# A hand-made TensorE order for 32 experts: the small products go into one block inside the next expert's first product

## The chip, the core and the metric

The kernel runs on one core of one Trainium2 chip. The metric is the device time of one execution in microseconds, as the median of several runs. A core has five engines with a queue of instructions each: TensorE (PE; its weight loads are shown as PEld), VectorE (DVE), ScalarE (ACT), GpSimd (POOL) and SyncE (SP), which here starts the loads. Each engine takes its own queue in order; between engines semaphores make one wait for another. TensorE reads SBUF and writes PSUM, which has eight banks of 128 partitions x 512 fp32 numbers; every tile of PSUM here is one bank.

## The reference

One decoder layer for 256 tokens of width 1024. A mixing part (gated DeltaNet, stick-breaking attention, cross-attention) comes first. The change touches the second part, a mixture of experts:

```python
logits = x @ w_router + b_router            # 32 experts, each token takes its best 4
gate = softmax(top 4 of logits)
for each expert e, for the tokens that chose it:
    hid = x @ w_gate_up[e] + b_gate_up[e]   # 1024 -> 2048
    glu, lin = min(hid[:, :1024], 7), clip(hid[:, 1024:], -7, 7)
    act = glu * sigmoid(1.702 * glu) * (lin + 1)
    y += gate * (act @ w_down[e] + b_down[e])   # 1024 -> 1024
x = layer_norm(2 ** 0.25 * x + y)
```

All is fp32. The weights of one expert are 12 MB (2 to the 20th bytes each), of all 32 experts 384 MB; each is read once.

## The kernel before

The mixing part takes about the first 355 us. The change is in what follows, the experts, in `tile_layer`.

**Loads.** The weights come in pieces of 128 partitions x 2048 numbers, 1 MB (1.0486 million bytes): eight for the first product of an expert (`wu`, one for each 128 rows of the 1024), four for the second (`wd`). SyncE starts them in a fixed order, the eight of expert e and then the four of expert e-1, into a ring of 21 buffers (`slots["ring"]`: tags of several pools, the last eight added just ahead of the experts). A load waits until the products that read its buffer's old piece are done. Line 829 issues them all.

**One expert.** It has 64 slots for tokens. With e the expert:

- `gather` makes, for two experts at a time (even e), `xg`: products of x with a 0/1 matrix `g2` put the chosen tokens' columns in place (`ps_xg`, two banks' worth, one after the other), and ScalarE and VectorE move each of eight slices out with LayerNorm's scale and bias. `xg` has one buffer for both experts.
- `gemm1` puts the biases into two banks, `glu` (`pg`) and `lin` (`pl`), through products with a selecting matrix `sel` (line 1169), and adds, for each of eight pieces, four products of 64 output partitions (line 1173). The 64 slots fill half of the array's columns, so the products go in pairs for the two halves of a bank; a pair runs side by side. The activation on VectorE and ScalarE follows (`eg`, `es`, `el`).
- `turned` transposes the activation (`pt`, copied to `aT`), and makes from ranks and gates the matrix `gT` and the column `gs` for the way back (`pq`). `pt` and `pq` share the bank `misc`, which has one buffer.
- `gemm2` puts the output bias into the bank `o` (`po`, line 1212) and adds the second product (line 1215), 16 products for four pieces. ScalarE and VectorE make of it the scaled halves `oh` and `ol`.
- `scatter` adds them to the tokens' rows: eight products `y` into four banks that stay for all experts (line 1230).

Experts 5 and 7 hold the residual as well (`residual`, `add_residual`), expert 31 the rows of the last LayerNorm (`ln2_rows`).

**What sets TensorE's order.** The loop at the end of the MoE part writes expert e's `gemm1` with two calls inside (`between`: `scatter(e-2)` behind the first piece, `turned(e-1)` behind the second), and then `gemm2(e-1)`. But a scheduler orders each engine's instructions by its own idea of their times, so what stands in TensorE's queue differs from the text and from expert to expert.

**The branch.** At e = 23 (`IFAT`), after the loads of expert 24 and `scatter(22)`, the kernel reads the largest number of tokens of an expert. If it is over 64, a loop handles the further slots; in these runs it is not. All engines stand at this branch until the others have come.

Of the kernel before, what the change touches and what calls it, by code (L numbers as in the profile page):

```python
# [17 lines left out]
P = 128  # L18
# [15 lines left out]
def tile_layer(ctx, tc, x, xT, memT, w_in, w_convT, a_log, dt_bias, gdn_norm_w, w_mem_kv, w_p_gdn, w_p_sb,  # L34
# [1100 lines left out]
    XG, ACT, SEL, TU, YO = {}, {}, {}, {}, {}  # L1135
# [5 lines left out]
    def gather(e, rcol):  # L1141
        g2 = ew.tile([P, 2, 2, 64], F32, name=f"g2_{e}", tag="g2")
# [6 lines left out]
        for q in range(2):  # L1149
            ps = psg.tile([P, 4, P], F32, name=f"ps_xg{e}{q}", tag=("misc", "o")[q])  # L1150
# [14 lines left out]
    def gemm1(e, sel, between=()):  # L1165
        pg = psg.tile([P, 512], F32, name=f"pg{e}", tag="glu")
        pl = psg.tile([P, 512], F32, name=f"pl{e}", tag="lin")
        for t, ps in enumerate((pg, pl)):
            nc.tensor.matmul(ps, sel, bias[:, t, :], start=True, stop=False)  # L1169
        outs = [(pg, 0), (pg, 1), (pl, 0), (pl, 1)]  # L1170
        for k in range(KT):
# [3 lines left out]
            if k < len(between):  # L1175
                between[k]()
# [32 lines left out]
    def gemm2(e, sel):  # L1209
        aT, gT, gs = TU.pop(e)  # L1210
        po = psg.tile([P, 512], F32, name=f"po{e}", tag="o")
        nc.tensor.matmul(po, sel, bias[:, 2, :], start=True, stop=False)  # L1212
        for ft in range(8):
            for h in range(2):
                nc.tensor.matmul(po[64 * h:64 * h + 64, :], aT[:, ft % 4, ft // 4, :],  # L1215
                                 WD[e][ft // 2].rearrange("p (a c) -> p a c", a=2)[:, ft % 2, 512 * h:512 * h + 512],
                                 start=False, stop=(ft == 7))
        oh = ew.tile([P, 512], F32R, name=f"oh{e}", tag="e3", bufs=3)
# [43 lines left out]
    def ln2_rows():  # L1262
# [4 lines left out]
        return ln2  # L1267
# [18 lines left out]
    def further_slots():  # L1286
# [16 lines left out]
        with tc.For_i(0, -(-T // cap) - 1, 1):  # L1303
            with tc.For_i(0, nexp, 1) as er:
# [15 lines left out]
                gather("o", rc[:, :, None].to_broadcast([P, 2, 2]))  # L1320
                gemm1("o", osel)
                WD["o"] = [down_piece("o", k, er) for k in range(4)]
                turned("o", rc, [gc[:, i:i + 1] for i in range(2)])
                gemm2("o", osel)
# [6 lines left out]
    for e in range(nexp + 1):  # L1331
        load(e)
        if e == IFAT:
            load(e + 1)
        if e < nexp:
            if e % 2 == 0:
                gather(e, rank[:, :, e:e + 2])
            SEL[e] = spread(brs[:, e, :], f"sel{e}")
            if e in (5, 7):
                residual((e - 5) // 2)  # L1340
            between = [lambda: scatter(e - 2)] if e - 2 in YO else []
            if e:
                between.append(lambda: turned(e - 1, rank[:, :, e - 1], [G[:, i, e - 1:e] for i in range(2)]))
            gemm1(e, SEL[e], between)
            if e in (5, 7):
                add_residual((e - 5) // 2)
        else:
            scatter(e - 2)
            turned(e - 1, rank[:, :, e - 1], [G[:, i, e - 1:e] for i in range(2)])
        if e == 0:  # L1350
            gates_of()
        if e == nexp - 1:
            ln2 = ln2_rows()
        if e:
            gemm2(e - 1, SEL[e - 1])
        if e == 2:
            rmi = largest_count()
        if e == IFAT:
            scatter(e - 1)
# [60 lines left out]
```

## Time and profile before

| | |
|---|---|
| median of 3 runs | 1327.99 us (1327.63 to 1331.89) |
| the profiled execution by its own time | 1330.67 us |
| its span in the trace | 1328.9 us |
| TensorE busy | 1262.2 us, 95% of the span |
| VectorE, ScalarE, GpSimd busy | 30%, 21%, 8% |
| bytes read from HBM | 451.35 MB |
| mean granted TensorE clock | 0.991 |

In the views an instruction has the line of the kernel, the engine, the operation, and the tiles out<-in by the program's names. A product of 64 output partitions shows as two records in the trace. In a timeline rows of one kind are merged (x4); in square brackets stands how long the engine was idle before the row and who ended that. In the table of waits, the waiter stands before the arrow and the one waited for behind it. GB/s counts all that the core's 16 DMA engines moved.

### The profile page before, as it was taken

To read this page: it belongs to the slowest core of one execution; us is meant where nothing else is said; L and a number is where in the kernel's file an instruction comes from. 1 tells how busy PE (TensorE), PEld (TensorE's weight loads), DVE (VectorE), ACT (ScalarE), POOL (GpSimd) and SP (SyncE) were. 2 spreads that over 40 slices of the span, in tenths; PEclk is the share of its full clock that TensorE was granted. 3 is DMA by queue.
4 is the path that set the end of the run, shared out by engine and by line. 5 is a ranking of instruction groups with operands and counts; after the bars stand their busy time and mean duration, and the time that the engine had idled before them with its cause. 6 is when DMAs were issued, how large, how long until landed. Compare 5 with 4: busy or idle time off the path is not lost. (4 is left out here: it accounts for less than half of the span.)

```text
span 1328.9 us, 16802 instructions
## 1 busy us (share of the span) xinstructions
PE 1262.2 (95%) x7039; PEld 682.1 (51%) x7039; DVE 400.3 (30%) x692; ACT 276.8 (21%) x448; POOL 99.8 (8%) x156
## 2 busy tenths in 40 slices
PE   7999999999999999999999999999999899999995
PEld 7998889999734433333333333333333244333331
DVE  6875646557412111111111111111121121111203
ACT  5565537445301101010100011010100011010111
POOL 4223313001000000000000000000000000000001
PEclk9999999999999999999999999999999999999998
DMA  7542337867699999999999999999999699999960
GB/s 238 177 142 74 117 135 224 305 191 289 258 418 422 424 422 423 421 413 415 422 420 419 422 424 424 421 423 422 422 423 424 263 389 422 425 421 424 423 278 32
DMA packets 117135, 453.54 MB, mean 341 GB/s; under 512 B 7440, under 2 KB 47456, under 8 KB 84288
## 3 DMA queue, kind: packets, MB, share of 16 engines
q1 hardware_dynamic: 116096, 450.39, 84.3%
q0 software_dynamic: 960, 2.04, 0.6%
q8 instruction: 57, 0.93, 0.3%
q14 instruction: 22, 0.18, 0.0%
HBM read 451.35 MB, written 1.05 MB: 340 GB/s over the span
## 5 line engine op out<-in xcount | busy, mean ns | idle before, releaser
L1173 PE MATMUL pg<-wu,xg 128*64 128x512 f32 x1024 | 316.3, 604 | 0.0
L1173 PE MATMUL pl<-wu,xg 128*64 128x512 f32 x1024 | 306.8, 593 | 0.0
L1215 PE MATMUL po<-wd,aT 128*64 128x512 f32 x1024 | 231.7, 597 | 0.0
L1173 PEld LDWEIGHTS pl<-wu,xg 128*64 128x64 f32 x1024 | 86.6, 137 | 145.8 <-issue 145.7
L1215 PEld LDWEIGHTS po<-wd,aT 128*64 128x64 f32 x1024 | 68.8, 136 | 127.3 <-issue 117.3
L1173 PEld LDWEIGHTS pg<-wu,xg 128*64 128x64 f32 x1024 | 75.7, 136 | 106.0 <-issue 87.5
L1180 DVE TENSOR_SCALAR eg<-pg 128x512 f32<-128x512 f32 x32 | 22.1, 692 | 341.9 <-PE pg L1173 341.9
L68 ACT ACTIVATE es<-eg 128x512 f32<-128x512 f32 x32 | 20.2, 631 | 470.0 <-DVE eg L1180 470.0
L1221 DVE SCALAR_TENSOR_TENSOR ol<-po,gs,oh 128x512 fp32r<-128x512 f32 x32 | 24.0, 750 | 219.9 <-ACT oh L1220 219.8
L1272 POOL CAST sel<-brs 128x128 fp32r<-128x128 f32 x32 | 11.4, 357 | 886.9 <-PE po L1212 886.3
L1154 PEld LDWEIGHTS ps_xg<-g,x 128*128 128x128 f32 x512 | 63.7, 201 | 27.7 <-issue 21.9
L1154 PE MATMUL ps_xg<-g,x 128*128 128x128 f32 x512 | 70.2, 291 | 2.9 <-DVE gs L1206 2.7
L1220 ACT ACTIVATE oh<-po,gs 128x512 fp32r<-128x512 f32 x32 | 22.0, 687 | 244.2 <-PE po L1215 244.2
L1204 DVE CAST gT<-pq 128x256 fp32r<-128x256 f32 x32 | 13.6, 424 | 147.2 <-PE pq L1202 147.2
L1230 PE MATMUL y<-oh,gT 64*128 64x512 f32 x128 | 34.5, 463 | 22.2 <-ACT oh L1220 22.2
L1230 PEld LDWEIGHTS y<-oh,gT 64*128 64x128 f32 x128 | 13.5, 184 | 68.6 <-ACT oh L1220 45.1
L1161 ACT ACTIVATE xg<-ps_xg,l1T 128x128 f32<-128x128 f32 x64 | 29.1, 454 | 77.3 <-PE ps_xg L1154 57.1
L1163 DVE TENSOR_SCALAR xg<-ps_xg,l1T 128x128 f32<-128x128 f32 x64 | 26.1, 408 | 35.7 <-ACT xg L1161 34.9
L1193 ACT COPY aT<-pt 128x512 f32<-128x512 f32 x32 | 18.6, 580 | 46.5 <-PE pt L1191 46.5
L1191 PEld LDWEIGHTS pt<-ident,el 128*128 128x128 f32 x128 | 13.4, 140 | 28.2 <-DVE xg L1163 9.7
L1230 PE MATMUL y<-ol,gT 64*128 64x512 f32 x128 | 27.6, 414 | 0.2
L1181 DVE TENSOR_SCALAR el<-pl 128x512 f32<-128x512 f32 x32 | 22.1, 691 | 5.3 <-PE pl L1173 5.3
(580 smaller groups left out, 1737.1 us busy)
## 6 DMA issues: line engine op xcount, KB each, us to landing
wu<-in_w_gate_up_dram SPq DMA_DIRECT2D x256, 1024.0 KB, 10.3
wd<-in_w_down_dram SPq DMA_DIRECT2D x127, 1024.0 KB, 11.1
wg<-in_w_in_dram SPq DMA_DIRECT2D x12, 1024.0 KB, 5.6
wo<-in_w_o_dram SPq DMA_DIRECT2D x4, 1024.0 KB, 5.1
wk<-in_w_in_dram SPq DMA_DIRECT2D x2, 1024.0 KB, 6.0
wv<-in_w_in_dram SPq DMA_DIRECT2D x2, 1024.0 KB, 5.2
wsq<-in_w_in_dram SPq DMA_DIRECT2D x2, 1024.0 KB, 5.8
wsk<-in_w_in_dram SPq DMA_DIRECT2D x2, 1024.0 KB, 5.1
```

Of the source, the lines that this page charges most:

```text
L68: o = nc.scalar.activation(out, in_, func, **kw)
L1154: nc.tensor.matmul(ps[:, k, :], x1[:, i, d * P:(d + 1) * P], g2[:, i].rearrange("p a b -> p (a b)"), start=(i == 0), stop=(i == 1))
L1161: nc.scalar.activation(dst, ps[:, k, :], AF.Identity, scale=g, bias=b)
L1163: nc.vector.tensor_scalar(dst, ps[:, k, :], g, b, op0=OP.mult, op1=OP.add)
L1173: nc.tensor.matmul(ps[64 * h:64 * h + 64, :], XG[e][:, k, :], WU[e][k][:, 512 * c:512 * c + 512], start=False, stop=(k == KT - 1))
L1180: nc.vector.tensor_scalar(g, pg, 7.0, None, op0=OP.min)
L1181: nc.vector.tensor_scalar(l, pl, 7.0, -7.0, op0=OP.min, op1=OP.max)
L1193: nc.scalar.copy(aT.rearrange("p j a b -> p j (a b)"), pt)
L1215: nc.tensor.matmul(po[64 * h:64 * h + 64, :], aT[:, ft % 4, ft // 4, :], WD[e][ft // 2].rearrange("p (a c) -> p a c", a=2)[:, ft % 2, 512 ...
L1220: nc.scalar.activation(oh, po, AF.Copy, scale=gs)
L1221: nc.vector.scalar_tensor_tensor(ol, po, gs, oh.bitcast(F32), op0=OP.mult, op1=OP.subtract)
L1230: nc.tensor.matmul(yps[i][h], gT[64 * h:64 * h + 64, i, :], o[64 * h:64 * h + 64, :], start=(e == 0 and n == 0), stop=(e == nexp - 1 and n ...
```

## The change

TensorE's queue is now written by hand: the loop stands in `tc.manual_schedule(engines={PE})`, which keeps TensorE's instructions in the order of the text; the other engines are ordered as before. The functions become generators, so that the loop can put one's work between the steps of another:

- Biases: `up_bias(e+1)` stands behind `gemm2(e-1)`, the output bias inside `turned`.
- One block behind the second weight piece of `gemm1(e)`: the transposes `pt`, `scatter(e-2)`, the output bias, `pq`. For e = 5 and 7 the scatter stands behind the first piece, with the residual.
- The gather for experts e+1 and e+2 (odd e): its first half ahead of `gemm2(e-1)`, the second behind that product's second weight piece. Both halves use `misc`; before, the second used `o`. The first gather, and the one behind the branch, stand undivided.
- `largest_count` moves from e = 2 to e = 0, `ln2_rows` between the pieces of the last `gemm1`.

```diff
-            ps = psg.tile([P, 4, P], F32, name=f"ps_xg{e}{q}", tag=("misc", "o")[q])
+            ps = psg.tile([P, 4, P], F32, name=f"ps_xg{e}{q}", tag="misc")
...
-    def turned(e, rc, gates):
+    def turned(e, sel, rc, gates, between=None):
         pt = psg.tile([P, 4, P], F32, name=f"pt{e}", tag="misc")
         for j in range(4):
             nc.tensor.transpose(pt[:, j, :], ACT[e][:, j * P:(j + 1) * P], ident)
+        if between:
+            between()
         aT = ew.tile([P, 4, 2, 64], F32, name=f"aT{e}", tag="e3", bufs=3)
         nc.scalar.copy(aT.rearrange("p j a b -> p j (a b)"), pt)
+        PO[e] = po = psg.tile([P, 512], F32, name=f"po{e}", tag="o")
+        nc.tensor.matmul(po, sel, bias[:, 2, :], start=True, stop=False)
...
+    with tc.manual_schedule(engines={mybir.EngineType.PE}):
...
+                for k in gemm1(e):
+                    if k == 0 and e in (5, 7):
+                        scatter(e - 2)
+                        residual((e - 5) // 2)
+                    if k == 1 and e:
+                        turn_down(e - 1)
...
+                if e % 2 and e + 1 < nexp and e != IFAT:
+                    nxt = pair(e + 1)
+                    next(nxt)
...
+                for k in gemm2(e - 1):
+                    if nxt and k == 1:
+                        next(nxt)
+            if e == IFAT:
+                scatter(e - 1)
+                with tc.If(nc.values_load(rmi[0:1, 0:1], min_val=0, max_val=T) > cap):
+                    further_slots()
+                for _ in pair(e + 1):
+                    pass
+            if e + 1 < nexp:
+                up_bias(e + 1, SEL[e + 1])
```

`turn_down(e)` calls `turned(e, ...)` with `scatter(e-1)` as `between`. Two places of TensorE's queue follow. First, behind the last piece of expert 9's first product. The names: `pg10`, `pl10` gate and linear sums of expert 10, `po8` the output of expert 8, `wd8_0` its first down piece, `ps_xg101` the second half of the gather for experts 10 and 11. Before:

```order
L1169 MATMUL pg10_5177<-bias_2348,sel10_5175 128x512
L1169 MATMUL pl10_5178<-bias_2348,sel10_5175 128x512
L1215 MATMUL po8_5100<-wd8_0_5020,aT8_5055 64x512 x4
L1191 MATMUL pt9_5197<-ident_133,el9_5094 128x128 x4
L1215 MATMUL po8_5100<-wd8_1_5022,aT8_5055 64x512 x4
L1215 MATMUL po8_5100<-wd8_2_5024,aT8_5055 64x512 x4
L1215 MATMUL po8_5100<-wd8_3_5026,aT8_5055 64x512 x4
L1230 MATMUL y00_3821<-oh8_5118,gT8_5064 128x512
L1230 MATMUL y01_3822<-oh8_5118,gT8_5064 128x512
L1230 MATMUL y10_3823<-oh8_5118,gT8_5064 128x512
L1173 MATMUL pg10_5177<-wu10_0_5122,xg_10_5148 64x512
L1154 MATMUL ps_xg101_5162<-g2_10_5146,x1_2139 128x128 x8
```

and now:

```order
L1155 MATMUL ps_xg100_5107<-g2_10_5104,x1_2139 128x128 x8
L1223 MATMUL po8_5059<-wd8_0_5028,aT8_5057 64x512 x4
L1223 MATMUL po8_5059<-wd8_1_5030,aT8_5057 64x512 x4
L1155 MATMUL ps_xg101_5130<-g2_10_5104,x1_2139 128x128 x8
L1223 MATMUL po8_5059<-wd8_2_5032,aT8_5057 64x512 x4
L1223 MATMUL po8_5059<-wd8_3_5034,aT8_5057 64x512 x4
L1170 MATMUL pg10_5155<-bias_2348,sel10_5120 128x512
L1170 MATMUL pl10_5156<-bias_2348,sel10_5120 128x512
L1178 MATMUL pg10_5155<-wu10_0_5159,xg_10_5106 64x512 x2
L1178 MATMUL pl10_5156<-wu10_0_5159,xg_10_5106 64x512 x2
L1178 MATMUL pg10_5155<-wu10_1_5161,xg_10_5106 64x512 x2
L1178 MATMUL pl10_5156<-wu10_1_5161,xg_10_5106 64x512 x2
```

The transposes `pt9` and the `y` of expert 8 no longer stand here; the gather stands whole around two pieces of the down product, and no gate product stands without its partner. Second, the first pieces of expert 10, where the rest of the small products stands. Before:

```order
L1230 MATMUL y11_3824<-oh8_5118,gT8_5064 128x512
L1230 MATMUL y00_3821<-ol8_5119,gT8_5064 128x512
L1230 MATMUL y01_3822<-ol8_5119,gT8_5064 128x512
L1230 MATMUL y10_3823<-ol8_5119,gT8_5064 128x512
L1230 MATMUL y11_3824<-ol8_5119,gT8_5064 128x512
L1173 MATMUL pg10_5177<-wu10_1_5124,xg_10_5148 64x512 x2
L1173 MATMUL pl10_5178<-wu10_1_5124,xg_10_5148 64x512 x2
L1200 MATMUL pq9_5204<-ident_133,gg9_5205 128x128 x2
L1202 MATMUL pq9_5204<-G_221,gg9_5205 128x1 x2
L1173 MATMUL pg10_5177<-wu10_2_5126,xg_10_5148 64x512 x2
L1173 MATMUL pl10_5178<-wu10_2_5126,xg_10_5148 64x512 x2
L1212 MATMUL po9_5247<-bias_2348,sel9_5028 128x512
```

and now:

```order
L1195 MATMUL pt9_5191<-ident_133,el9_5098 128x128 x4
L1240 MATMUL y00_3821<-oh8_5151,gT8_5068 128x512
L1240 MATMUL y01_3822<-oh8_5151,gT8_5068 128x512
L1240 MATMUL y10_3823<-oh8_5151,gT8_5068 128x512
L1240 MATMUL y11_3824<-oh8_5151,gT8_5068 128x512
L1240 MATMUL y00_3821<-ol8_5152,gT8_5068 128x512
L1240 MATMUL y01_3822<-ol8_5152,gT8_5068 128x512
L1240 MATMUL y10_3823<-ol8_5152,gT8_5068 128x512
L1240 MATMUL y11_3824<-ol8_5152,gT8_5068 128x512
L1201 MATMUL po9_5206<-bias_2348,sel9_4986 128x512
L1208 MATMUL pq9_5208<-ident_133,gg9_5209 128x128 x2
L1210 MATMUL pq9_5208<-G_221,gg9_5209 128x1 x2
```

Transposes, all eight `y` of expert 8, the output bias of expert 9 and `pq9` are one block between pieces 1 and 2.

## Rows read from the trace of the kernel before

**Rows 1.** The page: the span, and GB/s in its 40 slices.

```profile
span 1328.9 us, 16802 instructions
...
GB/s 238 177 142 74 117 135 224 305 191 289 258 418 422 424 422 423 421 413 415 422 420 419 422 424 424 421 423 422 422 423 424 263 389 422 425 421 424 423 278 32
```

**Rows 2.** Stages: length; busy us of PE, PEld, DVE, ACT, POOL; granted clock; DMA share; GB/s.

```profile
370.00:470.00 100.00, 99.97 (x488) 39.55 (x486) 21.04 (x43) 11.87 (x20) 0.89 (x3) 1.00 1.02 423
470.00:600.00 130.00, 125.02 (x589) 49.69 (x587) 23.55 (x46) 10.83 (x20) 1.48 (x5) 1.00 1.01 420
600.00:1045.00 445.00, 424.93 (x1985) 159.78 (x1983) 76.55 (x152) 38.94 (x73) 6.15 (x15) 1.00 1.02 422
1045.00:1075.00 30.00, 25.10 (x126) 12.68 (x122) 6.77 (x13) 3.73 (x7) 0.00 (x0) 0.89 0.52 210
1075.00:1275.00 200.00, 195.01 (x916) 73.65 (x917) 35.15 (x69) 18.15 (x33) 2.31 (x7) 1.00 1.02 423
1275.00:1329.00 54.00, 36.71 (x180) 14.59 (x176) 13.77 (x29) 6.38 (x10) 4.20 (x4) 0.90 0.24 94
```

**Rows 3.** Timeline of TensorE, 630 to 700: start us, us, then the instructions.

```profile
636.42 0.47 PE L1169 MATMUL pg<-bias,sel 128*128 128x512 f32 x1
...
646.29 0.73 PE L1230 MATMUL y<-oh,gT 64*128 64x512 f32 x3 [0.85 <-ACT oh L1220]
646.96 1.07 PE L1173 MATMUL pg<-wu,xg 128*64 128x512 f32 x2
647.96 2.05 PE L1154 MATMUL ps_xg<-g,x 128*128 128x128 f32 x16
...
666.40 0.47 PE L1169 MATMUL pg<-bias,sel 128*128 128x512 f32 x1
...
696.02 0.47 PE L1169 MATMUL pg<-bias,sel 128*128 128x512 f32 x1
```

**Rows 4.** Waits of the load queue, 700 to 1000: us in total, times, longest.

```profile
SPq L829 <- PE pl L1173: 173.1, 80, 6.2
```

**Rows 5.** Loads, 600 to 1000: count, KB each, median us from issue to landing.

```profile
wu<-in_w_gate_up_dram SPq DMA_DIRECT2D x111, 1024.0 KB, 9.5
```

**Rows 6.** Waits of the load queue, 1075 to 1275.

```profile
SPq L829 <- DMA wu<-in_w_gate_up_dram: 56.4, 35, 2.1
```

**Rows 7.** Loads, 1080 to 1260.

```profile
wu<-in_w_gate_up_dram SPq DMA_DIRECT2D x48, 1024.0 KB, 19.6
```

**Rows 8.** Timeline around the branch, 1045 to 1075, TensorE and the load queue.

```profile
1050.99 7.04 PE L1215 MATMUL po<-wd,aT 128*64 128x512 f32 x32
...
1064.21 4.51 SPq L829 DMA_DIRECT2D wu<-in_w_gate_up_dram  x8
...
1064.39 0.77 PE L1169 MATMUL pg<-bias,sel 128*128 128x512 f32 x1 [4.00 <-PEq L1360]
```

**Rows 9.** Timeline of TensorE, 1300 to 1329: the last down product.

```profile
1307.01 7.09 PE L1215 MATMUL po<-wd,aT 128*64 128x512 f32 x32
```

**Rows 10.** Timeline of TensorE, 400 to 460: experts 2 to 4.

```profile
403.48 0.48 PE L1169 MATMUL pg<-bias,sel 128*128 128x512 f32 x1
...
409.57 1.07 PE L1173 MATMUL pg<-wu,xg 128*64 128x512 f32 x2
410.57 0.44 PE L1200 MATMUL pq<-ident,gg 128*128 128x128 f32 x2
...
429.20 0.47 PE L1169 MATMUL pg<-bias,sel 128*128 128x512 f32 x1
...
458.47 0.48 PE L1169 MATMUL pg<-bias,sel 128*128 128x512 f32 x1
```

**Rows 11.** Timeline of TensorE, 1275 to 1290: a turnaround of `misc`.

```profile
1280.83 0.93 PE L1258 MATMUL ps_l<-lnr,ident 32*128 32x128 f32 x6 [0.68 <-ACT ln L1266]
```

**Rows 12.** The page, costliest groups: busy us, mean ns, idle before.

```profile
L1180 DVE TENSOR_SCALAR eg<-pg 128x512 f32<-128x512 f32 x32 | 22.1, 692 | 341.9 <-PE pg L1173 341.9
...
L1161 ACT ACTIVATE xg<-ps_xg,l1T 128x128 f32<-128x128 f32 x64 | 29.1, 454 | 77.3 <-PE ps_xg L1154 57.1
```

More of the change, by code (lines that the diff above doesn't have):

```diff
@@ L1163, in gather, with up_bias, gemm1 @@
                     nc.vector.tensor_scalar(dst, ps[:, k, :], g, b, op0=OP.mult, op1=OP.add)
[L1165 to L1168, printed above, removed]
+            yield
+    def up_bias(e, sel):
+        UP[e] = [psg.tile([P, 512], F32, name=f"p{nm}{e}", tag=tag) for nm, tag in (("g", "glu"), ("l", "lin"))]
+        for t, ps in enumerate(UP[e]):
             nc.tensor.matmul(ps, sel, bias[:, t, :], start=True, stop=False)
+    def gemm1(e):
+        pg, pl = UP.pop(e)
         outs = [(pg, 0), (pg, 1), (pl, 0), (pl, 1)]
@@ L1207, in turned, with gemm2 @@
         TU[e] = aT, gT, gs
-    def gemm2(e, sel):
+    def gemm2(e):
         aT, gT, gs = TU.pop(e)
-        po = psg.tile([P, 512], F32, name=f"po{e}", tag="o")
-        nc.tensor.matmul(po, sel, bias[:, 2, :], start=True, stop=False)
+        po = PO.pop(e)
         for ft in range(8):
@@ L1319, in further_slots @@
                 WU["o"] = [up_piece("o", k, er) for k in range(KT)]
-                gather("o", rc[:, :, None].to_broadcast([P, 2, 2]))
-                gemm1("o", osel)
+                up_bias("o", osel)
+                for _ in gather("o", rc[:, :, None].to_broadcast([P, 2, 2])):
+                    pass
+                for _ in gemm1("o"):
+                    pass
                 WD["o"] = [down_piece("o", k, er) for k in range(4)]
-                turned("o", rc, [gc[:, i:i + 1] for i in range(2)])
-                gemm2("o", osel)
+                turned("o", osel, rc, [gc[:, i:i + 1] for i in range(2)])
+                for _ in gemm2("o"):
+                    pass
                 scatter("o")
@@ L1329, in further_slots @@
         slots["ring"], cnt[0] = ring, c0
[L1331 to L1359, printed above, removed]
-            with tc.If(nc.values_load(rmi[0:1, 0:1], min_val=0, max_val=T) > cap):
-                further_slots()
@@ L1362, in tile_layer, with pair, turn_down @@
-    scatter(nexp - 1)
+    def pair(e):
+        return gather(e, rank[:, :, e:e + 2])
+    def turn_down(e):
+        turned(e, SEL[e], rank[:, :, e], [G[:, i, e:e + 1] for i in range(2)], (lambda: scatter(e - 1)) if e - 1 in YO else None)
+    with tc.manual_schedule(engines={mybir.EngineType.PE}):
+        SEL[0] = spread(brs[:, 0, :], "sel0")
+        up_bias(0, SEL[0])
+        for _ in pair(0):
+            pass
+        rows2 = ln2 = None
+        for e in range(nexp + 1):
+            load(e)
+            if e == IFAT:
+                load(e + 1)
+            nxt = None
+            if e < nexp:
+                for k in gemm1(e):
[4 more added lines that the diff above has]
+                        turn_down(e - 1)
+                    if e == nexp - 1 and 2 <= k < 6:
+                        rows2 = rows2 or ln2_rows()
+                        ln2 = next(rows2)
+                if e in (5, 7):
+                    add_residual((e - 5) // 2)
+                if e % 2 and e + 1 < nexp and e != IFAT:
+                    nxt = pair(e + 1)
+                    next(nxt)
+            else:
+                turn_down(e - 1)
+            if e + 1 < nexp:
+                SEL[e + 1] = spread(brs[:, e + 1, :], f"sel{e + 1}")
+            if e == 0:
+                gates_of()
+                rmi = largest_count()
+            else:
+                for k in gemm2(e - 1):
+                    if nxt and k == 1:
+                        next(nxt)
+            if e == IFAT:
+                scatter(e - 1)
+                with tc.If(nc.values_load(rmi[0:1, 0:1], min_val=0, max_val=T) > cap):
+                    further_slots()
+                for _ in pair(e + 1):
+                    pass
+            if e + 1 < nexp:
+                up_bias(e + 1, SEL[e + 1])
+        scatter(nexp - 1)
```

9 lines of the change are left out of this document (5 added, 4 removed).

## The prediction

> **What bounds the kernel now.** I read the page first, then the stages, then the queue that starts the transfers, then TensorE's order. The page [rows 1] shows the transfers near 422 GB/s from the twelfth of the 40 slices on, but with one dip to 263 late and an end of two slices with little traffic. The stages say more [rows 2]. From 370 to 470 us TensorE is busy 99.97 of 100 us and the transfers move 423 GB/s. From 600 to 1045 they move 422, and TensorE is busy for 425 of 445 us. Both look full, so neither share says which one sets the time. From 1045 to 1075, where the branch on the largest count stands, they move 210 on average. From 1275 on they are nearly done, while the kernel runs for 54 us more.
>
> An expert has 12 pieces of 1.0486 MB, 12.58 MB in all; at 423 GB/s that is 29.75 us. TensorE's own period, from one gate bias to the next, is 29.98 us and then 29.62 us, so 29.80 us (636.42, 666.40 and 696.02) [rows 3]. The two agree within 0.2%, and which of them is the limit must come from the queue of loads. Between 700 and 1000 us that queue waits for the products that free a buffer, 173.1 us in 80 waits for `pl` alone [rows 4], and a load lands 9.5 us after its issue [rows 5]. A piece takes 2.48 us at 423 GB/s, so fewer than four of the 21 buffers are in flight; the other 17 hold weights that have landed or are being used. So TensorE is the limit there, some 17 pieces behind the transfers. After the branch it differs: between 1075 and 1275 us the queue waits mostly for earlier transfers [rows 6], a load takes 19.6 us to land [rows 7], and the rate is 423. That is what the transfers can do with eight in flight: the floor under any faster TensorE.
>
> Being 17 pieces behind costs twice. At the branch SyncE waits until TensorE has done its work of expert 22, and after that expert's down weights only 12 pieces stand ahead of the branch. All have landed, so the transfers stop: 30 us at 210 instead of 423 GB/s is 15.1 us lost [rows 2]. The queue starts again at 1064.21 [rows 8]. At the end TensorE still works off its backlog, to 1307.01 + 7.09 = 1314.1 us [rows 9], long after the last load.
>
> **The change part by part.** *The order inside an expert.* Before, single products stand between the two halves of a pair. At 646.96 one gate product stands alone for 1.00 us, until 647.96 [rows 3], where four products take 1.76 us (32 records in 7.04 us, two records to a product) [rows 8]. The `y` products come right behind the down product and wait 0.85 us for ScalarE's `oh` [rows 3]. The block puts `y` behind two weight pieces of the next expert: 3.5 us of cover against that 0.85 us, so I cost this wait at nothing; were the cover gone, it would return at 0.85 us an expert.
>
> The price of the new order comes from the early experts, whose rows are already nearly in it [rows 10]: 25.72 us without a gather (403.48 to 429.20) and 29.27 with one (429.20 to 458.47). One flaw of theirs goes: at 409.57 half a pair stands alone and takes 1.00 us, until 410.57, where its share of a pair is 0.44, and the pairs behind it stay shifted until a last half is alone again. I estimate 0.9 us for both. The new order has no split pair: 24.8 and 28.4, and with 0.3 us for entering the down product again between the two gather halves, a mean of 26.7 us. If the flaw stays in another form the mean is 27.5; with nothing lost on entries it is 26.4. I take 26.7, 3.1 below 29.80.
>
> *One bank for both gather halves and the block.* The second half of `ps_xg` moves from the output's bank to `misc`, so it waits until four slices are moved out. Inside the down product two weight pieces, 3.5 us, cover this. At the first gather and after the branch nothing does. The nearest row is a turnaround of the same bank, 0.68 us behind ScalarE's copy [rows 11]; two slices on each of two engines take twice 0.45 us of moving [rows 12], so I estimate 1.5 us each (0 to 3). The first delays the first buffers freed, so it counts; the second comes while weights are queued. In the block, `pq` waits for the copy of `pt`; `y` and the output bias, about 1.5 us, cover it, except for experts 5 and 7, where the wait is under 1 us twice and falls on a TensorE that catches up anyway. Output bias and next gate biases stand where their banks have long been read. Loads keep their order, the other engines their work.
>
> *What is late next.* 3.1 us of TensorE's time per expert is not 3.1 us of the kernel's: the floor of 29.75 us stays. TensorE gains on the transfers, 12 x (1 - 26.7 / 29.75) = 1.2 pieces per expert, and has used up its 17 pieces after 14 experts, a few more with the residual of experts 5 and 7. From about expert 18 it waits for weights, some 3 us an expert. The branch then comes with pieces still on their way: the transfers run on unless TensorE is more than 12 - 6.2 / 2.48 = 9.5 pieces behind (6.2 us is from the end of the down product at 1058.03 to the queue's restart) [rows 8]. So the 15.1 us go. SyncE reaches the branch only when it has issued expert 23's last piece, so TensorE may wait for it there, and the gather follows; I estimate nine pieces of arrears, which seven experts at 1.2 make good.
>
> **The sum.** What is moved after 370 us [rows 2]: 100 x 423 + 130 x 420 + 445 x 422 + 30 x 210 + 200 x 423 + 54 x 94, less 1.05 MB of output, is 379.6 MB. At 423 GB/s without a stop that is 897.5 us, so the last weights land at 1267.5 us, with 1.5 for the first gather at 1269. Behind them TensorE has one piece, 1.8 us, and is 1.5 us late from the last block, whose `y` waits for `oh` with no cover: 1272.3. From the last down product to the end stays 1328.9 - 1314.1 = 14.8 us [rows 1, 9]: span 1287.1. The profiled execution took 1330.67 us by its own time, 1.8 over its span, which makes 1288.9; the median of the runs, 1327.99, lies 2.7 below it. So 1286 to 1287 for the median; I take 1287, -3.1%. The saving of 41 us is 15 at the branch and the rest at the end, where TensorE no longer has a backlog.
>
> **A rule against it.** A window with a wait of 4.00 us at the branch shows a granted clock of 0.89, the long stretch with 0.85 us waits in every expert shows 1.00 [rows 2, 3, 8]. Waits for pieces would be 2.48 - 1.76 = 0.7 us each, so by these rows the clock stays at 2.4 GHz. The Trainium skill, "TensorE: Matmul & The Clock Gate", section "HAM oscillation — how this bites in real kernels", tells of a kernel whose wait for each weight slice put the clock back to its lower level every time. That is a rival here, priced from rows: at 1.2 GHz a piece takes 3.5 us, 1.0 more than its transfer; TensorE falls behind, so its waits end and the clock can rise again. Only the last 12 pieces can cost, up to 12 us.
>
> **The rivals.**
> 1. TensorE gains too little: half-pairs or bank waits of 2 us come back in each expert, the period is 28.7. Then it catches up 0.4 pieces per expert and is over 9.5 behind at the branch. What counts is TensorE alone: 1.1 us for the experts whose period is near 29.80 (15 from 600 to 1045 us, an estimated 23 in all) is 25 us, so 1304. For it: every turnaround in [rows 3, 11]. Against: the cover counted above.
> 2. Nothing is gained, since the transfers are already at their rate: 1325 to 1331. For it: 422 against 423 GB/s [rows 2] and the near-equal periods. It would mean that TensorE stays behind, that is, that the change doesn't do what it says. Against: [rows 4, 5].
> 3. Slower: the fixed order puts each turnaround of `misc` bare on TensorE's path. `pt` to `pq` and the two gather halves share the bank, 0.9 us for the first and, with VectorE's four operations of the activation (0.69 us each) [rows 12] ahead of the moves, 3.7 us in every second expert for the others. With 0.85 for `y` that is 3.6 us on 26.7, a period of 30.3: 0.5 us over 23 experts is 12 us, so 1340. It decides once the waits exceed 3.1 us per expert. Against: 3.5 us of down product stand between the halves.
> 4. The clock rule above: 1298.
>
> **How the numbers follow.** Forecast 0.72, rival 1 0.11, rival 2 0.06, rival 3 0.06, rival 4 0.05. A measurement tells a change of 0.3% from none. Faster by more: forecast and rivals 1 and 4, 0.88; within: 0.06; slower: 0.06. The range: 423 GB/s may be 0.5% more or less, 4.5 us; the first gather costs 0 to 3; TensorE's last part 2 to 6. Low 1280; high 1304, which takes in rivals 1 and 4.
>
> **What would show it.** Right: from about the middle on, TensorE's idle time ends on loads of `wu` and `wd`, loads take some 20 us to land, SyncE waits for earlier transfers; no dip at the branch; the last load near 1269 us and the last down product within 5 us of it; early periods of 24.8 and 28.4. Wrong: a dip near 1050 us, `pq` or `ps_xg` waiting in each expert, a clock under 1.00 between 700 and 1000 us, or a rate well off 423 GB/s.

## The result, and the profile after

The median of four runs is 1295.87 us (1293.91 to 1298.6) against 1329.19 us for the kernel before, run beside it: a ratio of 0.9749, 95% interval 0.9721 to 0.9777. The forecast was 1287 us, the range 1280 to 1304. So the sign and most of the size came as forecast, and 9 us were missing. The profiled execution took 1294.32 us by its own time; its span is 1292.6 us against a forecast of 1287.1, which is where the miss can be looked for.

The page after: span, GB/s in 40 slices, the head of the chain that ended last, and two of the costliest groups (busy us, mean ns, then idle time ahead and its cause).

```profile
span 1292.6 us, 16782 instructions
...
GB/s 245 179 148 66 116 130 213 323 195 241 310 320 423 422 423 424 422 424 423 422 424 421 423 422 422 425 423 422 423 422 425 422 343 425 422 424 421 422 425 210
...
DMA wu<-in_w_gate_up_dram 4%; PE po L1223 3%; DMA wd<-in_w_down_dram 3%; PE pg L1178 2%; PE pl L1178 2%; PE ps_xg L1155 1%; PE y L1240 0%; PE ps_l L1268 0%; PE pt L1195 0%; DVE bsb L1404 0%; DVE x L1421 0%; PE po L1201 0%; PE pg L1170 0%; PE pq L1210 0%; PE pq L1208 0%; DVE ol L1231 0%
...
L1178 PE MATMUL pg<-wu,xg 128*64 128x512 f32 x1024 | 268.7, 603 | 16.4 <-DMA wu<-in_w_gate_up_dram 16.2
...
L1223 PE MATMUL po<-wd,aT 128*64 128x512 f32 x1024 | 234.3, 598 | 15.8 <-DMA wd<-in_w_down_dram 15.8
```

Against [rows 1] the rate is 421 to 425 from the thirteenth slice on but for one of 343, the branch, and the loads go on into the last slice (210). TensorE's idle time now ends on transfers: 16.2 us ahead of `pg`, 15.8 ahead of `po`. The stages, with the columns of [rows 2]:

```profile
600.00:1020.00 420.00, 398.44 (x1959) 154.40 (x1957) 77.61 (x151) 40.68 (x72) 4.40 (x15) 1.00 1.02 423
1020.00:1075.00 55.00, 45.12 (x216) 20.80 (x214) 9.16 (x20) 5.01 (x9) 0.59 (x2) 0.88 0.91 377
1075.00:1245.00 170.00, 159.88 (x786) 61.50 (x782) 30.57 (x58) 16.91 (x30) 1.47 (x5) 1.00 1.02 423
1245.00:1293.00 48.00, 33.96 (x173) 13.95 (x172) 13.77 (x29) 6.37 (x10) 4.19 (x4) 0.90 0.68 276
```

From 600 to 1020 TensorE is busy for 398.44 of 420 us, 95% as before, at a granted clock of 1.00, and the transfers move 423 GB/s: the shares tell nothing of a change. The stretch around the branch shows 377 GB/s: 55 us x (1 - 377 / 423) = 6.0 us of transfers lost there. The waits of the load queue from 700 to 1000 us (us in total, times, longest), the counterpart of [rows 4]:

```profile
SPq L829 <- DMA wu<-in_w_gate_up_dram: 93.5, 57, 2.1
SPq L829 <- DMA wd<-in_w_down_dram: 80.4, 40, 2.5
SPq L829 <- PE pl L1178: 49.3, 29, 3.1
```

173.9 us on earlier transfers and 49.3 on `pl`, where it was 173.1 on `pl` alone. That is what [rows 6] showed behind the branch. A load of the stretch from 600 to 1000 us lands 19.7 us after its issue; before, it was 9.5 there [rows 5] and 19.6 behind the branch [rows 7]:

```profile
wu<-in_w_gate_up_dram SPq DMA_DIRECT2D x106, 1024.0 KB, 19.7
```

Now TensorE's timeline in four places: the first gather, two experts early on, a down product late with the branch, and the end with TensorE's last wait for a weight.

```profile
354.60 3.66 PE L1155 MATMUL ps_xg<-g,x 128*128 128x128 f32 x16
360.20 2.05 PE L1155 MATMUL ps_xg<-g,x 128*128 128x128 f32 x16 [1.93 <-DVE xg L1164]
362.18 1.08 PE L1178 MATMUL pg<-wu,xg 128*64 128x512 f32 x4
...
626.63 0.50 PE L1170 MATMUL pg<-bias,sel 128*128 128x512 f32 x1
...
650.89 0.50 PE L1170 MATMUL pg<-bias,sel 128*128 128x512 f32 x1
...
679.43 0.50 PE L1170 MATMUL pg<-bias,sel 128*128 128x512 f32 x1
...
1017.21 1.94 PE L1223 MATMUL po<-wd,aT 128*64 128x512 f32 x8 [0.51 <-DMA wd<-in_w_down_dram]
...
1032.41 3.75 PE L1155 MATMUL ps_xg<-g,x 128*128 128x128 f32 x16 [5.99 <-PEq L1391]
1038.15 3.53 PE L1155 MATMUL ps_xg<-g,x 128*128 128x128 f32 x16 [1.98 <-DVE xg L1164]
1041.43 0.48 PE L1170 MATMUL pg<-bias,sel 128*128 128x512 f32 x1
...
1240.54 1.08 PE L1178 MATMUL pg<-wu,xg 128*64 128x512 f32 x4 [0.44 <-DMA wu<-in_w_gate_up_dram]
...
1270.70 7.09 PE L1223 MATMUL po<-wd,aT 128*64 128x512 f32 x32
```

The first gather, in the kernel before:

```profile
355.89 5.33 PE L1154 MATMUL ps_xg<-g,x 128*128 128x128 f32 x32 [0.25 <-DVE g L1143]
361.15 1.08 PE L1173 MATMUL pg<-wu,xg 128*64 128x512 f32 x4
```

The gate biases of three experts stand 24.26 and 28.54 us apart; at 1017.21 a down product waits 0.51 us for its piece; at the branch TensorE stands for 5.99 us, and the gather behind it waits 1.98 us for its own bank; the last down product ends at 1277.8, 36.3 us earlier than before [rows 9], with 14.8 us behind it, as before. From 1240.54 to there TensorE waits for no weight any more: these 37.25 us are its own work on the pieces that have come in time.

The queue's side of the branch, timeline and waits from 1020 to 1075:

```profile
1027.06 8.22 SPq L829 DMA_DIRECT2D wd<-in_w_down_dram  x3
1053.60 4.02 SPq L829 DMA_DIRECT2D wu<-in_w_gate_up_dram  x8
```

```profile
SPq L1391 <- SPq L1391: 16.9, 3, 11.8
```

The last piece ahead of the branch is issued by 1035.28 and the next at 1053.60: 18.3 us, of which 16.9 are waits that the branch's own line holds. TensorE had gone on at 1032.41, so the engines do not all stand here until the others have come, as the section on the kernel before puts it. The same wait of the queue stood in the trace before, shorter (1040 to 1075):

```profile
SPq L829 <- PEq L1360: 10.9, 1, 10.9
SPq L1360 <- SPq L1360: 8.9, 3, 3.8
```

### The profile page after: what moved, and what is told of

The parts are those of the page before. It is cut to its first block, busy times and chain, and to the rows that moved or that the text cites. A ratio compares the mean times of both kernels' runs of the same rounds, so it can differ in the third digit from the quotient of the medians.

```text
span 1292.6 us, 16782 instructions
## 1 busy us (share of the span) xinstructions
PE 1219.3 (94%) x7039; PEld 676.8 (52%) x7039; DVE 403.1 (31%) x692; ACT 280.4 (22%) x448; POOL 97.8 (8%) x156
## 5 line engine op out<-in xcount | busy, mean ns | idle before, releaser
L1178 PE MATMUL pg<-wu,xg 128*64 128x512 f32 x1024 | 268.7, 603 | 16.4 <-DMA wu<-in_w_gate_up_dram 16.2
L1178 PE MATMUL pl<-wu,xg 128*64 128x512 f32 x1024 | 263.2, 592 | 0.0
L1223 PE MATMUL po<-wd,aT 128*64 128x512 f32 x1024 | 234.3, 598 | 15.8 <-DMA wd<-in_w_down_dram 15.8
L1178 PEld LDWEIGHTS pl<-wu,xg 128*64 128x64 f32 x1024 | 73.7, 137 | 146.1 <-issue 146.1
L1178 PEld LDWEIGHTS pg<-wu,xg 128*64 128x64 f32 x1024 | 63.9, 136 | 147.2 <-issue 83.6
L1240 PE MATMUL y<-oh,gT 64*128 64x512 f32 x128 | 23.4, 444 | 1.9 <-ACT oh L1230 1.9
L1188 DVE TENSOR_TENSOR el<-el,es 128x512 f32<-128x512 f32 x32 | 22.2, 692 | 3.6 <-ACT es L68 0.5
L1187 DVE SCALAR_TENSOR_TENSOR el<-el,eg 128x512 f32<-128x512 f32 x32 | 22.1, 692 | 1.1
## 6 DMA issues: line engine op xcount, KB each, us to landing
wu<-in_w_gate_up_dram SPq DMA_DIRECT2D x256, 1024.0 KB, 19.6
wd<-in_w_down_dram SPq DMA_DIRECT2D x127, 1024.0 KB, 19.7
```

Of the source, the lines that this page charges most:

```text
L1178: nc.tensor.matmul(ps[64 * h:64 * h + 64, :], XG[e][:, k, :], WU[e][k][:, 512 * c:512 * c + 512], start=False, stop=(k == KT - 1))
L1187: nc.vector.scalar_tensor_tensor(l, l, 1.0, g, op0=OP.add, op1=OP.mult)
L1188: nc.vector.tensor_tensor(l, l, s, OP.mult)
L1240: nc.tensor.matmul(yps[i][h], gT[64 * h:64 * h + 64, i, :], o[64 * h:64 * h + 64, :], start=(e == 0 and n == 0), stop=(e == nexp - 1 and n ...
```

## The experiments

Each ratio is to the kernel before, run beside it on the same chip; `m` is the median.

| kernel | m, us | ratio, 95% | profiled span |
|---|---|---|---|
| changed kernel, measured three times | 1295.87, 1294.35, 1294.64 | 0.9749, 0.9716, 0.9736 | 1292.6, 1292.8, 1298.3 |
| changed, no branch | 1292.67 | 0.9711, 0.9681 to 0.9742 | 1293.0 |
| before, no branch | 1328.96 | 1.0001, 0.9983 to 1.002 | 1326.9 |
| changed, two gathers on two banks | 1292.48 | 0.972, 0.9688 to 0.9752 | 1288.4 |
| and the loads not taken from GpSimd | 1288.17 | 0.969, 0.9655 to 0.9725 | 1286.8 |
| the same again | 1288.16 | 0.97, 0.9679 to 0.972 | 1284.8 |
| changed, transposes three times | 1296.9 | 0.9739, 0.9705 to 0.9774 | 1296.3 |
| changed, transposes nine times | 1360.46 | 1.0221, 1.0195 to 1.0247 | 1361.5 |
| before, its text's order held | 1303.61 | 0.9778, 0.9744 to 0.9813 | 1303.9 |
| changed, order left to the scheduler | 1321.39 | 0.9926, 0.9896 to 0.9956 | 1320.2 |

**The branch taken out of the changed kernel.** The further slots are left out; no expert here has any.

```diff
-                with tc.If(nc.values_load(rmi[0:1, 0:1], min_val=0, max_val=T) > cap):
-                    further_slots()
```

> The kernel after, without the branch on the largest count and its path for further slots (left out; these inputs do not need it). Theory A (weights set the time, and the branch empties the load queue: SyncE waits there for its eight loads in flight, so the transfers pause): the pause of 6.0 us between 1046.9 and 1057.9 us goes and nothing else changes, so a span of 1286 to 1287 against 1292.6, ratio to before 0.969 to 0.971. Rival B (the missing time is TensorE's: its stop of 6.0 us at the branch and the undivided gather behind it leave it late to the end): 12 to 15 us go, a span near 1279, ratio 0.964. Rival C (the branch costs nothing any more; what the forecast missed lies elsewhere): 1291 to 1293, ratio 0.975.

```profile
1020.00:1075.00 55.00, 49.75 (x250) 19.92 (x248) 8.60 (x18) 5.01 (x9) 0.59 (x2) 1.00 1.02 423
```

```profile
362.12 2.46 PE L1155 MATMUL ps_xg<-g,x 128*128 128x128 f32 x16 [1.93 <-DVE xg L1164]
364.51 1.98 PE L1178 MATMUL pg<-wu,xg 128*64 128x512 f32 x4
```

From 1020 to 1075 us the transfers now run at 423 GB/s, so the pause belongs to the branch. The ratio, 0.9711, is the one expected, but it lies no lower than one of the changed kernel's three, 0.9716; the span, 1293.0, is not the one expected. From 340 to 380 us the transfers moved 274 GB/s where the changed kernel moved 307, which at 423 is 40 x 33 / 423 = 3.1 us lost before the gain began. Of this 1.9 us are a gather that starts later (356.53 against 354.60), which the edit does not touch. The rest, 1.2, is the clock behind the gather's wait: the first weight products take 1.98 us for four records, where the changed kernel's take 1.08, at a granted clock of 0.50 from 364 to 366 us against 1.00.

The rest of the 6.0 us does not show in the span either. What had been moved by 1240 us, first here and then in the changed kernel:

```profile
DMA packets 113667, 439.04 MB, mean 354 GB/s; under 512 B 7147, under 2 KB 47163, under 8 KB 81435
```

```profile
DMA packets 113549, 438.19 MB, mean 353 GB/s; under 512 B 7134, under 2 KB 47150, under 8 KB 81422
```

By bytes this run is 0.85 MB ahead, 2.0 us. But the second piece of expert 31, for which TensorE waits in both, comes at the same time (its product starts at 1240.58 and 1240.54), and the transfers thin out earlier, at 280 GB/s from 1268 to 1272 us against 409. Why the lead is in other pieces than the one that is needed, no run shows.

**The branch taken out of the kernel before**, by the same edit.

> The kernel before, without the branch and its path for further slots (left out). Theory A (TensorE sets the time before; the transfers' pause of 15.1 us at the branch is no loss of its own): only TensorE's stop goes, 4.0 us of idle and 2 to 3 us at the lower clock behind it, so 1321 to 1323 in span, ratio 0.994 to 0.996. Rival (the transfers set the time, as the forecast's split of the saving into 15 at the branch and the rest at the end has it): the 15.1 us go, 1313 to 1314, ratio 0.988.

```profile
1045.00:1075.00 30.00, 28.78 (x141) 11.00 (x139) 6.15 (x13) 3.52 (x7) 0.29 (x1) 1.00 1.02 421
...
1275.00:1326.00 51.00, 34.77 (x171) 13.63 (x169) 12.94 (x26) 6.38 (x10) 4.20 (x4) 0.92 0.06 21
```

The 210 GB/s of [rows 2] became 421, almost nothing is left to load at the end (21 GB/s), and the time stayed: 1.0001. The last down product starts at 1304.73, 2.3 us earlier than in [rows 9], but the gate bias of expert 1 stood 3.5 us earlier already (371.60 against 375.13). This pair alone does not price the pause, since the order changed too: expert 23, at the branch, became 10.5 us shorter (29.63 against 40.13), while the four behind it became 11.7 longer, as the scheduler gave them periods of 28.7 to 30.0 us where two of the kernel before had 25.7 and 21.1. That also took back the 5 us expected of TensorE's stop. What shows that the pause cost nothing is the trace of the kernel before: from 370 us to the end its TensorE does not wait for a single weight, so a transfer that comes earlier is worth nothing to it.

**Two banks for the gathers that stand undivided.**

```diff
-            ps = psg.tile([P, 4, P], F32, name=f"ps_xg{e}{q}", tag="misc")
+            ps = psg.tile([P, 4, P], F32, name=f"ps_xg{e}{q}", tag=("misc", "o" if e in (0, IFAT + 1) else "misc")[q])
```

> The kernel after, with the second half of the two undivided gathers (the first one, and the one behind the branch) in the output's bank again, so that it needs no wait for the moves of the first half. Theory A: the first landing behind the full ring comes 2 to 3 us earlier (gap 10.18 us in the kernel after, 7.28 in the one before), and as weights set the time to the end all of it is kept: span 1289.5 to 1291, ratio 0.972 to 0.974. Behind the branch it changes TensorE's time alone, hidden. Rival (a TensorE start that is late by 2 us is made good like any other lateness of TensorE): 1292 to 1293, ratio 0.975.

The span is 4.2 us under the changed kernel's, a little better than expected. Of this 2.1 us are a gather that starts earlier (352.46 against 354.60), which the edit does not touch; the first weight product then comes 4.96 us behind the gather's start and not 7.58, 2.6 us. Of the medians, 1292.48 against 1294.35 to 1295.87, one cannot tell so small a step alone. The transfers around the branch are as before the edit, 374 GB/s.

**The same, and the loads of the path not taken issued from GpSimd.** SyncE's program says why its queue stands at a branch that is not taken. On the path that skips the further slots stands a wait for each of the eight counters of SyncE's own loads, shown here at the jump that ends the path:

```
L1391 TENSOR_LOAD rmi [waits DVE_49]
L1391 COMPARE_AND_BRANCH
...
L1391 UNCONDITIONAL_BRANCH [waits DMAHW0_49,DMAHW1_49,DMAHW2_49,DMAHW3_49,DMAHW4_49,DMAHW5_49,DMAHW6_49,DMAHW7_49]
```

The other path issues loads on the same counters. If these come from GpSimd, the eight waits are gone from SyncE's program:

```diff
+        q = nc.gpsimd if name.startswith(("wuo", "wdo")) else nc.sync
...
-            nc.sync.dma_start(v[:, a * w:(a + 1) * w], src[:, a * w:(a + 1) * w])
+            q.dma_start(v[:, a * w:(a + 1) * w], src[:, a * w:(a + 1) * w])
```

> As e3, and the loads of the path for further slots (never taken here) are issued by GpSimd instead of SyncE, so that at the branch SyncE has no loads to account for on the path not taken and does not wait for the eight in flight. Theory A: the pause of 6.0 us at the branch goes on top of e3: span 1283.5 to 1285.5, ratio 0.967 to 0.969, and no gap over 4 us between landings after 370 us. Rival (SyncE's 18 us between its last load ahead of the branch and the first behind it is the branch itself, such as fetching code behind the queued weights): the pause stays, 1289.5 to 1291.

And once more, with the changed kernel beside it:

> The changed kernel with the second half of the first gather and of the one behind the branch in the output's bank, and with the loads of the path not taken issued from GpSimd, so that SyncE does not wait for its loads in flight at the branch; the same text as measured before at 1288.17 us. Expected on this chip: 1286.5 to 1289.5 us, ratio 0.967 to 0.970, and 5 to 7.5 us under the changed kernel of the same call; if the two pauses of the transfers (6.0 at the branch, 2.9 at the first gather) are not what the forecast missed, the difference is under 3 us.

> The changed kernel unaltered, for the difference to the kernel with the two mended waits on one chip: 1293 to 1296 us, ratio 0.972 to 0.975.

Stretch around the branch, and timeline of the first gather and of the one behind the branch, in the second of these runs:

```profile
1020.00:1075.00 55.00, 47.41 (x234) 21.60 (x232) 9.16 (x20) 5.01 (x9) 0.59 (x2) 0.91 1.02 421
```

```profile
352.07 5.36 PE L1156 MATMUL ps_xg<-g,x 128*128 128x128 f32 x32
357.36 1.08 PE L1179 MATMUL pg<-wu,xg 128*64 128x512 f32 x4
...
1029.07 6.42 PE L1156 MATMUL ps_xg<-g,x 128*128 128x128 f32 x32 [6.21 <-PEq L1392]
```

421 GB/s where it was 377, with the branch in its place and TensorE standing there for 6.21 us all the same; SyncE's next load follows the last one ahead of the branch after 1.5 us (1030.91 to 1032.38). The first gather takes 5.29 us to the first weight product, as before the change, and not 7.58. Medians of 1288.17 and 1288.16 us; the changed kernel beside the second, 1294.64: 6.5 us. The intervals of these two ratios, 0.9679 to 0.972 and 0.972 to 0.9752, touch, so the size is loose, the sign is not: each of these nine runs lies under all three medians of the changed kernel. The spans, 1286.8 and 1284.8, lie 0.3 and 2.3 us under the 1287.1 of the forecast.

Spans compare these kernels badly, since the mixing part ahead ends at other times in each profile. What lies behind the first gather can be compared from the gate bias of expert 1 on:

| kernel | gate bias of expert 1 | span | difference |
|---|---|---|---|
| changed, three profiles | 376.16, 376.40, 381.73 | 1292.6, 1292.8, 1298.3 | 916.4, 916.4, 916.6 |
| two banks | 371.40 | 1288.4 | 917.0 |
| no branch | 379.72 | 1293.0 | 913.3 |
| two banks, loads from GpSimd, two profiles | 373.23, 371.34 | 1286.8, 1284.8 | 913.6, 913.5 |

With the pause 916.4 to 917.0, without it 913.3 to 913.6: the pause takes 6.0 us from the transfers and 3.1 us from the time. TensorE's stop, which the kernel without the branch does not have, makes no difference here.

**The same order with more work for TensorE.** The transposes `pt` are done three times, and in a second kernel nine times; the results do not change.

```diff
-        for j in range(4):
+        for j in [*range(4)] * 3:
```

> The changed kernel with the four transposes of the gates' columns (pt, in the block inside the first products of the next expert) done three times over: eight more single products per expert, an estimated 1.2 us more of TensorE's work per expert and 38 us in all; the results are the same. Theory A (the transfers set the time from about the middle on, TensorE waits there): the extra work fills waits; mean period of the early experts 27.6 instead of 26.4 us, TensorE catches up some ten experts later, and the kernel loses 0 to 3 us, ratio to the kernel before 0.974 to 0.980. Rival B (TensorE still sets the time, its own order is what got shorter): the 38 us show in full, ratio 1.00 to 1.005.

> The changed kernel with the four transposes of the gates' columns done nine times over: 32 more single products per expert. At the 0.11 us that each of them added to a period in the kernel with three times (0.86 us for eight) that is 3.44 us per expert and a mean period of 29.85 us, what the kernel before had, while every other part of the change stays. Theory A (the gain is TensorE's shorter period against the floor of 29.75 us of the transfers, and nothing else): TensorE never catches up, the branch pauses the transfers for 12 us or more, and the time goes back to that of the kernel before: ratio 0.99 to 1.005, span 1318 to 1332. Rival B (part of the gain is from elsewhere, the gather's place or the branch's): ratio 0.975 to 0.988.

Three times: the early periods are 25.14 and 29.41 us, mean 27.3, so 0.86 us more per expert; over 32 experts that is 27.5 us of TensorE's work, and the median rose by 2.6 us over the changed kernel beside it, 1294.35. The rest went where the changed kernel waited for pieces; TensorE caught up at expert 20, five later and not ten. Nine times:

```profile
631.43 0.50 PE L1170 MATMUL pg<-bias,sel 128*128 128x512 f32 x1
...
663.46 0.50 PE L1170 MATMUL pg<-bias,sel 128*128 128x512 f32 x1
...
691.22 0.50 PE L1170 MATMUL pg<-bias,sel 128*128 128x512 f32 x1
```

```profile
SPq L829 <- PE pl L1178: 174.2, 80, 7.6
```

The periods are 32.03 and 27.76, mean 29.90 us, and the queue waits for products again, 174.2 us, like [rows 4]. But the kernel is slower than before, 1360.46, which neither theory had. The expectation took the 29.80 of the middle for all of the kernel before; its early experts had 25.72 [rows 10] and two behind the branch 25.7 and 21.1, while this kernel pays 29.90 everywhere. What the pair shows stands: 8 added products cost a tenth of their time, 32 three fifths of theirs (3.5 x 32 = 112 us of work, 66 us of time), since past the floor everything counts.

**The order held, without the change; and the change, without the order held.** The kernel before with its loop inside `manual_schedule`, and the changed kernel with that line replaced.

```diff
-    for e in range(nexp + 1):
+    with tc.manual_schedule(engines={mybir.EngineType.PE}):
+        for e in range(nexp + 1):
...
```

```diff
-    with tc.manual_schedule(engines={mybir.EngineType.PE}):
+    if True:
```

> The kernel before, its text unaltered, but with its loop's order on TensorE held as written: no pair is split, the gates' transposes stand behind the first weight piece and the y products too, the gather of two experts stands undivided ahead of their first product. Theory A (what counts is that no half-pair stands alone and y has a cover; the exact places count little): mean period of the early experts 27 to 27.6 us, caught up before the branch, span 1290 to 1298, ratio 0.972 to 0.980. Rival B (the block's place two pieces in, and the gather split across the down product, are what makes the gain): period 29 or more, ratio 0.985 to 1.00.

> The changed kernel's text, but its loop's order on TensorE left to the scheduler instead of held: 14 half-pairs stand alone again, and y stands right behind the down product, where ScalarE's oh is not ready. Theory A (the held order makes the gain): period of the early experts some 28 us, caught up only near the branch, span 1297 to 1306, ratio 0.978 to 0.986. Rival B (the new text makes the gain by its blocks and banks, held or not): ratio 0.972 to 0.977 as with the changed kernel. Rival C (nothing is left of the gain): ratio 0.995 to 1.005.

The old text, held, has periods of 25.44 and 29.06 us, mean 27.25, catches up at expert 19 and gains 0.0222. Its span misses the upper bound by 6 us, and its end shows why: four groups of transposes for the last LayerNorm stand ahead of the last but one down product in one row, all but the first waiting 0.68 us for the bank.

```profile
1258.81 1.15 PE L1258 MATMUL ps_l<-lnr,ident 32*128 32x128 f32 x8
1260.64 1.15 PE L1258 MATMUL ps_l<-lnr,ident 32*128 32x128 f32 x8 [0.68 <-ACT ln L1266]
1262.46 2.07 PE L1258 MATMUL ps_l<-lnr,ident 32*128 32x128 f32 x8 [0.68 <-ACT ln L1266]
1265.21 2.07 PE L1258 MATMUL ps_l<-lnr,ident 32*128 32x128 f32 x8 [0.68 <-ACT ln L1266]
...
1267.93 9.24 PE L1215 MATMUL po<-wd,aT 128*64 128x512 f32 x32
...
1281.85 7.09 PE L1215 MATMUL po<-wd,aT 128*64 128x512 f32 x32
```

From 1258.81 to the down product at 1267.93 pass 9.1 us, and that product takes 9.24 us for its 32 records, not 7.04; in the changed kernel these groups lie between weight pieces. The last down product ends at 1288.9, 11.1 us later than there. So the block and the split gather are not needed for most of the gain, and `ln2_rows` between the pieces is worth most of the difference at the end, by the trace alone; that was not tried by itself.

The new text, left to the scheduler, keeps a gain of 0.7%, less than the first theory had and a little more than the third. Its order is split up again, and the periods in the middle are 29.45 and 29.86:

```profile
636.58 0.49 PE L1170 MATMUL pl<-bias,sel 128*128 128x512 f32 x1 [0.30 <-DVE el L1185]
...
648.29 0.73 PE L1240 MATMUL y<-oh,gT 64*128 64x512 f32 x3 [0.85 <-ACT oh L1230]
...
682.27 0.68 PE L1155 MATMUL ps_xg<-g,x 128*128 128x128 f32 x4 [0.67 <-DVE gs L1214]
```

```profile
600.00:1020.00 420.00, 398.51 (x1886) 151.19 (x1884) 72.62 (x145) 37.14 (x70) 4.15 (x14) 1.00 1.02 423
```

```profile
SPq L829 <- PE pl L1178: 144.7, 75, 3.5
```

Per expert 0.85 us ahead of `y`, 0.30 behind a gate bias, 0.67 in every second gather: 1.5 of the 3.25 us by which its mean of 29.65 is above 26.4. Of the other 1.8 a part is more entries to products (a down product in four parts of 1.94 us takes 7.76, undivided 7.04 [rows 8]); the rest was not counted out. Now compare its stretch from 600 to 1020 us with that of the changed kernel: 398.51 and 398.44 us busy, 423 and 423 GB/s. By these views they are one kernel; the table of waits tells them apart, 144.7 us on `pl` here and 173.9 on transfers there.

**The changed kernel again**, unaltered, beside these:

> The changed kernel once more, unaltered, as the yardstick for the other three on the same chip. Both theories expect a ratio of 0.972 to 0.977 and a profiled span of 1288 to 1294 us; if the gap in the landings behind the full ring varies from 8 to 12 us between profiles of one program, the spans of these kernels cannot be told apart by less than some 3 us.

## Why the prediction was right, and where it was not

- **What bounds it before**: right. TensorE of the kernel before waits for no weight from 370 us on, and with the change the queue's waits turned round as forecast.
- **TensorE's period**: 24.8 and 28.4 forecast, 28.7 with the entry, against 24.26 and 28.54. The mean is 26.4, not 26.7. The working names 26.4 for "nothing lost on entries", but its own 24.8 and 28.4 make 26.6; the measured mean comes from the expert without a gather, shorter by 1.46 than [rows 10] and not by 0.9. `y` waited 1.9 us in the whole kernel, where 0.85 us an expert stood before.
- **Catching up**: 14 experts at the least and "about expert 18" forecast; from expert 15 to the branch the periods are 28 to 31 us. The forecast's 1.2 pieces per expert are 1.35 at 26.4. Behind the branch three experts made the arrears good, of 23.64, 28.53 and 25.20 us, where seven were estimated.
- **The floor**: 422 or 423 GB/s held in every stretch from 370 to 1245 us without the branch.
- **The step that failed is "So the 15.1 us go".** Its condition was met: TensorE had no arrears. But the queue does not pass the branch when TensorE has come; it passes when its own eight loads in flight have landed. With TensorE behind, these landed while the queue had to wait for TensorE anyway, which it did for 10.9 us behind the branch's own 8.9; without arrears its own loads are what is late next. 6.0 us of transfers stay lost, shown by taking the branch out (no pause) and by taking that wait out with the branch in place (no pause); in the time this is 3.1 us. The row with 8.9 us on the branch's own line could be read before. Nor did TensorE wait for SyncE there: it went on at 1032.41, while SyncE still issued its last load.
- **The first gather**: 1.5 us taken, 0 to 3 given. The first weight product came 7.58 us after the gather's start, not 5.26: 2.3 us. The wait itself was 1.93, and two banks took it away. The sum has no term for the clock behind it. In the kernels with one bank the products behind the wait ran for a while at the lower level, 1.2 GHz (granted clock 0.50 from 360 to 362 us in the changed kernel measured again), in five profiles of six; expert 0 took 23.95 to 24.29 us there, 22.66 in the profile above, which is the sixth, and 20.20 before. With two banks TensorE does not stop, the clock is 1.00 from 360 us on, and expert 0 takes 20.02 to 20.51. So the wait cost 2.5 to 4.1 us.
- **The sum**: the span was 5.5 us over. By the gate biases of experts 0 and 1 the experts began 1.4 us earlier than in the kernel before (353.50 against 354.93), expert 0 took 1.0 more than the 20.20 and 1.5 forecast, and from there to the end it was 916.4 us, where the forecast leaves 1287.1 - 354.93 - 20.20 - 1.5 = 910.5: 6.0 more. Of these 3.1 go with the pause. The other 2.9 stay in the kernels without it, and their cause is open: the sum lets every byte count at 423 GB/s, while the lead in bytes of the kernel without the branch did not bring the piece that was needed any earlier. That 6.0 is also what the transfers lost at the branch is a coincidence of the numbers.
- **The end** came out near its terms, 14.8 us behind the last down product and 2.3 from the last load to the end of that product, forecast 3.3, but not by the path of the sum. The last load lands at 1275.5 us, not 1269 (100 GB/s from 1274 to 1276 us, 0 behind), and TensorE does not wait for it: its last wait for a weight ends at 1240.54, and 37.25 us of its own work follow.
- **"15 at the branch and the rest at the end"** was wrong as an account. The pause alone was worth nothing; all of the gain came from TensorE's period, and the transfers could use only as much of it as they did not lose.
- **From span to median**: forecast 1.9 us under the profiled execution's own time, measured 1.55 over it; that is 3.4 of the 8.9 us between 1287 and 1295.87. Part of it may be that the profiled execution has the shortest first gather of the six; the runs do not settle it.
- **The signs**: idle time on loads, 19.7 us to landing, and early periods came as said. Of the signs of being wrong one came too, the dip near 1050 us, and the last load was 6.5 us late.
- **The rivals**: no mean period of 28.7 and no bare turnaround in the experts (1, 3), and the time moved (2). The clock stayed at 1.00, 2.4 GHz, through waits of 0.51 us at each piece (4); the lower level came behind the single stops, at the first gather and at the branch. The Trainium skill, "TensorE: Matmul & The Clock Gate", section "HAM oscillation — how this bites in real kernels", tells of waits of some 3 to 5 us at each slice; such waits no stretch of experts here has, and at the branch, where TensorE stood for 5.99 us, the next 16 gather products took 3.75 us and later ones 2.05.

## What to carry to other kernels

When two limits are nearly equal, busy shares and GB/s read the same on either side; look at whom the queue of loads waits for, and how many pieces stand between it and its user. A shorter period of the slower one pays until the backlog is gone, and what was hidden under the backlog comes out then: list, ahead of the change, each wait of the load queue that is now covered, also the one that ends a branch not taken. And an order that a scheduler makes is part of the kernel: the same text held and not held were 27 us apart.

## What the runs showed of the hardware and the program that was not expected

- A branch that is not taken held the load queue for 18.3 us, until its eight loads had landed, and the transfers lost 6.0 us, the kernel 3.1; with the loads of the other path on another engine's queue there was no pause.
- A load issued into a full set of transfers lands 19.7 us after its issue and the rate is 423 GB/s; with fewer than four under way (9.5 us) it was 422. The rate alone does not tell how full the queue is.
- Behind the single wait of 1.93 us in the first gather the granted clock fell to 0.50 for some products in five of six profiles; with two banks, without the wait, it was 1.00 there in three of three.
- TensorE's stop at the branch was 3.69 to 4.00 us in the three kernels whose TensorE comes late there, and 5.95 to 6.21 in seven profiles of kernels that had caught up, with the pause of the loads and without it. The kernel with the transposes three times had caught up too and stood for 0.63 us, so what sets this stop is open:

```profile
1030.43 3.63 PE L1155 MATMUL ps_xg<-g,x 128*128 128x128 f32 x16 [0.63 <-PEq L1391]
```
